# A hybrid SSD and retention block: squares on two engines, transposes in two parts, earlier weight loads, mixed rows behind passes, a halved last bank

## The chip, the core and the metric

The kernel runs on one core of a Trainium2 chip. The metric is the device time of one execution in microseconds (us). The engines of the core work side by side, each through its own queue in order, and wait for one another by semaphores: TensorE (PE in the profile: matrix products; PEld is its weight load), VectorE (DVE), ScalarE (ACT), GpSimd (POOL) and SyncE (SP, which here only issues DMAs). PSUM has eight banks of 128 x 512 f32 numbers in which PE accumulates.

## The reference

One layer on 512 tokens of width 2048, batch 1. All in f32:

```python
mod = silu(c) @ w_ada + b_ada                  # shift, scale, gate
u = rms_norm(x, norm_w) * (1 + scale) + shift
z, xbc, dt_raw, q, k, v, g = split(u @ w_in)   # 2048 x 11296
# SSD: conv of 4 taps and SiLU on xbc; 32 heads, 4 groups, chunks of 128
y_ssd = group_rms_norm((ssd_chunked(xs, softplus(dt_raw + dt_bias), a, bm, cm) + xs * d_skip) * silu(z))
# retention: 8 heads, rotary q and k, decay per head, chunks of 128
y_ret = head_group_norm(retention_chunked(rot(q), rot(k), v)) * silu(g)
h = x + gate * (concat(y_ssd, y_ret) @ w_out)  # 4096 x 2048
return rms_norm(h, final_norm_w)
```

## The kernel before

Every large product is done in three matmuls on numbers that are split in two: a value is cast to a rounded part `hi` (ACT), the rest `lo` is the difference (DVE or POOL), and `mm3` (L107 to L109) adds hi·hi, hi·lo and lo·hi in PSUM. The layer goes through these stages.

**Start-up.** SP loads x as eight tiles `xt` of 128 x 1024 (four row blocks `t`, two halves `h`). ACT squares each with a sum (L158), POOL makes a factor of each row block of the two sums (L160, L75, L76), DVE scales the two tiles (L163), PE transposes (L168) into one PSUM bank for each of 16 blocks `k` of the width, banks of the tags "mm" and "aux" (four each) in turn, and ACT copies the bank to `xT` (L171). `csb` (L137 to L143) is silu(c) on all partitions.

**Modulation.** For each of the 16 blocks `mod` takes two dot products `dot` (L189): DVE multiplies a 1 MB tile `ada` of the modulation matrix, 128 x 2048, with `csb` and sums. ACT reads the sums (L199, L200), applies shift and scale to `xT` (L202) and casts it to `uh` (L205); DVE takes the rest `ul` (L206).

**The split phase.** The first products begin while the modulation is still under way. Two groups of columns, A (B and C of groups 0 and 1, and half of xs 0) and B (z 0 and the other half of xs 0), each fill six banks, four "mm" and two "aux". So they take turns over the pairs of blocks that are ready, as PLAN (L32) lists them: B0, then A0 A1, B1 B2, A2 A3 A4, B3 B4 B5, A5 A6 A7, B6 B7. `seg` does the products of one pair. Behind a turn `spill` (L264) copies the six banks to SBUF (`pA`, `pB`), and the group's next turn copies them back (L234). `weights` loads a pair's two tiles with `load_w`: SP's DMA to `raw` (3 buffers), a cast to `hi` on ACT (L98; 128 x 1024 for z or B and C, 128 x 512 for xs; 4 buffers), and `lo` on POOL, for late pairs on DVE (L99).

**SSD and retention.** A `unit` is a pass: a product of all 16 blocks with 512 columns. Between passes the four SSD groups (`ssd_a`, `ssd_b`) and the four pairs of retention heads run. Each gives four blocks of rows of the mixed matrix, which `put_mix` transposes on PE into a bank `pT` (L339), copies to `m` on ACT (L341, ring "mo" of three), combines on POOL (L349 to L352) and stores in DRAM with five POOL DMAs. During a pass `trickle` (SSD) and `between` (retention) put other small jobs behind its weight loads. `block_sums` prepares sums of w_out in DRAM by DMA.

**Output phase.** The product with w_out is done by a scheme of seven products on half-size blocks: three sweeps over banks U and W, and a last loop (L846 to L855) that adds the product with T4 to U's four banks, one for each pair (q, t) of column and row half. Its last three weight tiles are held and then used bank by bank. `finish` (L723) multiplies a bank with the gate, adds x and squares (L731 to L734); `store` (L739) makes the factor of a row block (L742, L75, L76), scales its four tiles on DVE (L747) and ACT (L749), and stores them.

A scheduler sets the order on each engine: it takes the program's order with priorities and its own model of times, and so an engine's queue isn't simply the order in which the code is written. `issue_after` ties one instruction behind another.

## Time and profile before

| | before |
|---|---|
| median of 3 runs | 1471.01 us (1468.2 to 1472.3) |
| profiled execution, its own time | 1466.36 us |
| its span from first to last instruction | 1464.7 us |
| mean clock granted to TensorE | 0.992 |
| DVE, ACT, POOL busy | 59%, 40%, 26% |
| start-up, to the first product of the split phase | 32.67 us |
| last matmul begins | 1453.13 us |

A row of the timeline has its start and its length in us, engine, line, operation, tiles (output<-inputs), shapes and count; in brackets stands how long the engine was idle before it, and what released it. A row with x2 or more has several instructions. A matmul of 128 x 512 is shown with 0.39 us, but the next one starts 0.23 us after it: they overlap.

### The profile page before, as it was taken

To read this page: it belongs to the slowest core of one execution; us is meant where nothing else is said; L and a number is where in the kernel's file an instruction comes from. 1 tells how busy PE (TensorE), PEld (TensorE's weight loads), DVE (VectorE), ACT (ScalarE), POOL (GpSimd) and SP (SyncE) were. 2 spreads that over 40 slices of the span, in tenths; PEclk is the share of its full clock that TensorE was granted. 3 is DMA by queue.
4 is the path that set the end of the run, shared out by engine and by line. 5 is a ranking of instruction groups with operands and counts; after the bars stand their busy time and mean duration, and the time that the engine had idled before them with its cause. 6 is when DMAs were issued, how large, how long until landed. Compare 5 with 4: busy or idle time off the path is not lost.

```text
span 1464.7 us, 17212 instructions
## 1 busy us (share of the span) xinstructions
PE 1427.2 (97%) x6481; PEld 1169.5 (80%) x6481; DVE 861.6 (59%) x1008; ACT 579.1 (40%) x820; POOL 380.7 (26%) x440
## 2 busy tenths in 40 slices
PE   6999999899999999999999999999999999999996
PEld 4777888788888888888888888888888778888885
DVE  6888657866556555543554355435535556558585
ACT  7666543434424423221322132213222456446453
POOL 4433114566035335501430143023200300000000
PEclk9999999999999999999999999999999999999999
DMA  9997643566647847966697578666644698778755
GB/s 363 349 362 265 221 178 118 177 197 167 188 156 210 243 144 215 280 221 180 215 262 235 158 228 263 228 156 198 184 153 154 212 329 268 245 242 271 238 185 189
DMA packets 86262, 324.09 MB, mean 221 GB/s; under 512 B 11297, under 2 KB 11473, under 8 KB 81057
## 3 DMA queue, kind: packets, MB, share of 16 engines
q1 hardware_dynamic: 67858, 262.30, 51.3%
q0 software_dynamic: 17168, 58.59, 17.1%
q10 hardware_dynamic: 1152, 2.10, 0.4%
q8 instruction: 51, 0.84, 0.2%
q14 instruction: 33, 0.27, 0.1%
HBM read 304.00 MB, written 86.05 MB: 266 GB/s over the span
## 4 chain that ended last, share of the span: by engine, by line
PE 82%; issue 5%; DMA 5%; ACT 3%; DVE 3%; POOL 2%; SPq 0%; DVEq 0%; POOLq 0%; ACTq 0%
PE acc L109 17%; PE acc L107 17%; PE acc L108 17%; PE U L107 3%; PE U L109 3%; PE U L108 3%; PE W L109 2%; PE W L108 2%; PE W L107 2%; PE py L442 2%; PE A L107 1%; DMA raw<-w_out_d 1%; PE A L108 1%; DMA ada<-w_mod_d 1%; PE A L109 1%
## 5 line engine op out<-in xcount | busy, mean ns | idle before, releaser
L98 ACT CAST hi<-raw 128x1024 fp32r<-128x1024 f32 (+1 forms) x184 | 186.8, 1016 | 446.8 <-PE acc L109 221.5
L99 DVE TENSOR_TENSOR lo<-raw,hi 128x1024 fp32r<-128x1024 f32 (+1 forms) x166 | 212.4, 1285 | 226.5 <-ACT hi L98 226.0
L108 PE MATMUL acc<-lo,uh 128*128 128x512 f32 x704 | 277.2, 394 | 0.0
L107 PE MATMUL acc<-hi,uh 128*128 128x512 f32 x704 | 276.0, 394 | 0.0
L109 PE MATMUL acc<-hi,ul 128*128 128x512 f32 x704 | 275.4, 392 | 0.0
L109 PE MATMUL acc<-uh,lo 128*128 128x512 f32 x512 | 201.0, 393 | 0.0
L108 PE MATMUL acc<-ul,hi 128*128 128x512 f32 x512 | 200.1, 391 | 0.0
L107 PE MATMUL acc<-uh,hi 128*128 128x512 f32 x512 | 199.7, 392 | 0.0
L774 DVE TENSOR_TENSOR lo<-raw,hi 128x1024 fp32r<-128x1024 f32 x112 | 137.9, 1235 | 83.4 <-ACT hi L773 83.1
L773 ACT CAST hi<-raw 128x1024 fp32r<-128x1024 f32 x112 | 117.8, 1054 | 128.1 <-PE W L109 52.1
L108 PEld LDWEIGHTS acc<-lo,uh 128*128 128x128 f32 x704 | 132.8, 189 | 27.8 <-issue 0.5
L109 PEld LDWEIGHTS acc<-hi,ul 128*128 128x128 f32 x704 | 132.6, 188 | 28.0 <-issue 0.5
L107 PEld LDWEIGHTS acc<-hi,uh 128*128 128x128 f32 x704 | 132.8, 189 | 27.6 <-ACT cr L306 0.3
L109 PEld LDWEIGHTS acc<-uh,lo 128*128 128x128 f32 x512 | 96.2, 188 | 20.1 <-issue 0.7
L107 PEld LDWEIGHTS acc<-uh,hi 128*128 128x128 f32 x512 | 96.2, 188 | 20.0 <-issue 0.7
L108 PEld LDWEIGHTS acc<-ul,hi 128*128 128x128 f32 x512 | 96.2, 188 | 19.6
L613 DVE SCALAR_TENSOR_TENSOR gacc<-graw,cs,gacc 128x512 f32<-128x512 f32 x60 | 47.5, 792 | 90.9 <-DMA graw<-w_gate_d 90.1
L108 PE MATMUL U<-lo,mh 128*128 128x512 f32 x256 | 100.0, 391 | 0.5 <-DVE lo L774 0.5
L109 PE MATMUL U<-hi,ml 128*128 128x512 f32 x256 | 99.6, 390 | 0.0
L107 PE MATMUL U<-hi,mh 128*128 128x512 f32 x256 | 95.5, 391 | 0.1
L189 DVE SCALAR_TENSOR_TENSOR ada<-ada,csb 128x2048 f32<-128x2048 f32 x32 | 90.5, 2855 | 0.8 <-DMA ada<-w_mod_d 0.8
L75 POOL TENSOR_SCALAR rs<-rs 128x1 f32<-128x1 f32 x4 | 2.1, 522 | 283.6 <-DVE rs L742 283.5
(238 smaller groups left out, 2255.2 us busy)
## 6 DMA issues: line engine op xcount, KB each, us to landing
ada<-w_mod_d SPq DMA_DIRECT2D x32, 1024.0 KB, 7.1
T<-w_out_d SPq DMA_DIRECT2D x64, 512.0 KB, 5.8
raw<-T SPq DMA_DIRECT2D x64, 512.0 KB, 4.3
raw<-w_out_d SPq DMA_DIRECT2D x48, 512.0 KB, 4.4
raw<-w_in_z SPq DMA_DIRECT2D x32, 512.0 KB, 4.1
T<-w_out_d POOLq DMA_DIRECT2D x32, 512.0 KB, 8.7
T<-T POOLq DMA_DIRECT2D x32, 512.0 KB, 14.7
raw<-w_in_qk SPq DMA_DIRECT2D x32, 512.0 KB, 4.2
```

The lines of the kernel that those rows point to most:

```text
L75: pool.tensor_scalar(dst, src, scale, eps, ALU.mult, ALU.add)
L98: act.copy(hi, raw)
L99: eng.tensor_tensor(lo, raw, hi.bitcast(F32), ALU.subtract)
L107: pe.matmul(dst, lhsT=ah, rhs=bh, start=first, stop=False, skip_group_check=more)
L108: pe.matmul(dst, lhsT=ah, rhs=bl, start=False, stop=False, skip_group_check=more)
L109: pe.matmul(dst, lhsT=al, rhs=bh, start=False, stop=last, skip_group_check=more)
L189: dve.scalar_tensor_tensor(ada, ada, 0.5, csb, ALU.mult, ALU.mult, accum_out=dst)
L442: pe.matmul(py[:, hd], lhsT=dec[:, h, :], rhs=xd[:, hd], start=True, stop=True)
L613: dve.scalar_tensor_tensor(gacc, raw[:, kk, :], cs[:, k:k + 1], gacc, ALU.mult, ALU.add)
L773: act.copy(dst[0], src)
L774: dve.tensor_tensor(dst[1], src, dst[0].bitcast(F32), ALU.subtract)
```

## The change

There are five parts.

1. Squares of the second half-tiles (h = 1) go from ACT to DVE, each half with its own `junk` buffer.
2. The transposes become a function `transposed(k)`: eight of them, then the first modulation and the weights of B0, whose cast is tied behind the first `uh` cast, and then the other eight.
3. The weights of the next turn's first pair are loaded in the code before the turn's spills.
4. The mixed rows of the SSD groups go to a list, `to_mix`; `mix_one` takes one off in the passes that follow, from their third weight tile on. The last two blocks `m` come from the ring "cbt".
5. In the last loop five weight tiles are held (LATE), the last bank is done in two halves of 256 columns, and row block 3 has finishing code of its own.

```diff
...
 ADAB = 4
 RING = 12
 EPS = 1e-6
+LATE = 5
 PLAN = [("B", [0]), ("A", [0, 1]), ("B", [1, 2]), ("A", [2, 3, 4]),
         ("B", [3, 4, 5]), ("A", [5, 6, 7]), ("B", [6, 7])]
 COL_Z, COL_XS, COL_B, COL_C, COL_DT = 0, 2048, 4096, 4608, 5120
...
 
     last_load = [None]
 
-    def load_w(src, width, eng=dve):
+    def load_w(src, width, eng=dve, after=None):
         raw = wp.tile([P, 2, width], F32, tag="raw", bufs=3, name="raw")
         last_load[0] = sp.dma_start(raw.rearrange("p k f -> p (k f)"), src)
         hi = wp.tile([P, 2, width], F32R, tag="hi", bufs=4, name="hi")
         lo = wp.tile([P, 2, width], F32R, tag="lo", bufs=4, name="lo")
-        act.copy(hi, raw)
+        with tc.issue_after(after) if after is not None else nullcontext():
+            act.copy(hi, raw)
         eng.tensor_tensor(lo, raw, hi.bitcast(F32), ALU.subtract)
         return hi, lo
 
...
     rst = const.tile([P, NC], F32, name="rst")
     for t in range(NC):
         for h in range(2):
-            junk = sp0.tile([P, HD], F32, tag="junk", bufs=1, name="junk")
-            act.activation(junk, xa[t][h], AF.Square, accum_out=ss[:, t, h:h + 1])
+            junk = sp0.tile([P, HD], F32, tag=f"junk{h}", bufs=1, name="junk")
+            if h == 0:
+                act.activation(junk, xa[t][h], AF.Square, accum_out=ss[:, t, h:h + 1])
+            else:
+                dve.scalar_tensor_tensor(junk, xa[t][h], 1.0, xa[t][h], ALU.mult, ALU.mult,
+                                         accum_out=ss[:, t, h:h + 1])
         r = rst[:, t:t + 1]
         pool.tensor_tensor(r, ss[:, t, 0:1], ss[:, t, 1:2], ALU.add)
         rsqrt_into(r, r, 1.0 / D, EPS)
         for h in range(2):
             dve.tensor_scalar(xa[t][h], xa[t][h], r, None, ALU.mult)
     xT = []
-    for k in range(NK):
+
+    def transposed(k):
         pt = bank("mm" if k % 2 else "aux", "pt")
         for t in range(NC):
             pe.transpose(pt[:, t * P:(t + 1) * P],
...
         ada = sp0.tile([P, D], F32, tag="ada", bufs=ADAB, name="ada")
         sp.dma_start(ada, w_mod[2 * k + m])
         dve.scalar_tensor_tensor(ada, ada, 0.5, csb, ALU.mult, ALU.mult, accum_out=dst)
+
+    last_split = [None]
 
     def mod(k0, nk):
 
...
             act.activation(xT[k], xT[k], AF.Identity, bias=sh, scale=sc)
             h_k = up.tile([P, L], F32R, tag="uh", bufs=NK, name=f"uh{k}")
             l_k = up.tile([P, L], F32R, tag="ul", bufs=NK + 1, name=f"ul{k}")
-            act.copy(h_k, xT[k])
+            last_split[0] = act.copy(h_k, xT[k])
             dve.tensor_tensor(l_k, xT[k], h_k.bitcast(F32), ALU.subtract)
             uh.append(h_k)
             ul.append(l_k)
...
 
     early = {}
 
-    def weights(which, p):
-        return [load_w(w_in[nm][p], wd, lo_eng(which, p)) for n, (nm, wd) in enumerate(ranges[which])]
+    def weights(which, p, after=None):
+        return [load_w(w_in[nm][p], wd, lo_eng(which, p), after)
+                for n, (nm, wd) in enumerate(ranges[which])]
 
     def seg(which, p, first, last):
         again = first and part[which][0] is not None
...
             act.copy(part[which][b], cur[which][b])
 
     plan = PLAN
+    for k in range(NK // 2):
+        transposed(k)
     mod(0, 1)
-    early["B", 0] = weights("B", 0)
+    early["B", 0] = weights("B", 0, last_split[0].ins)
+    for k in range(NK // 2, NK):
+        transposed(k)
     mod(1, 1)
     ready = 1
     last_of = {w: max(i for i, (v, _) in enumerate(plan) if v == w) for w in "AB"}
...
                 ready += 1
             seg(which, p, j == 0, j == len(pairs) - 1)
         if i != len(plan) - 1:
+            nxt = plan[i + 1][0], plan[i + 1][1][0]
+            early[nxt] = weights(*nxt)
             spill(which)
     start.close()
 
...
         return ap.rearrange("p (h d) -> p h d", h=HPG)
 
     half_of = {}
+    to_mix = []
+
+    def mix_one(kc):
+
+        if kc >= 2 and to_mix:
+            put_mix(*to_mix.pop(0))
 
     def put_mix(i, src, nw):
 
...
         pT = bank("aux", "pT")
         for c in range(NC):
             pe.transpose(pT[:, c * P:(c + 1) * P], src[c], ident)
-        m = t2k("mo", 3, "m")
+        m = t2k("cbt", 2, "m") if i >= 30 else t2k("mo", 3, "m")
         act.activation(m, pT, AF.Copy, scale=nw)
         if i % 2 == 0:
             half_of["m"] = m
...
     def trickle(kc):
         if kc % 2:
             copy_one()
+        mix_one(kc)
 
     def block_sums():
 
...
             act.activation(zss[c], y, AF.Square, accum_out=sq[:, c:c + 1])
             rsqrt_into(sq[:, c:c + 1], sq[:, c:c + 1], 1.0 / 2048.0, EPS)
             dve.tensor_scalar(y, y, sq[:, c:c + 1], None, ALU.mult)
-        for i in range(4):
-            put_mix(4 * g + i, [y[:, i * P:(i + 1) * P] for y in ys], hv(V_SNW, 4 * g + i))
+        to_mix.extend((4 * g + i, [y[:, i * P:(i + 1) * P] for y in ys], hv(V_SNW, 4 * g + i))
+                      for i in range(4))
 
 
     def rotary(pb, name):
...
             gate_part(i // 24, i // 3 % 8)
         else:
             copy_one()
+        mix_one(kc)
 
     def gate_part(n, q):
         raw = wp.tile([P, 2, 512], F32, tag="raw", bufs=3, name="graw")
...
         if j % 2 == 0:
             m = mixed(mixd["A22"][j // 2])
         held.append((j, m, weight(T4(j))))
-        if NJ - 3 <= j < NJ - 1:
+        if NJ - LATE <= j < NJ - 1:
             continue
         for at in PAIRS:
-            for j_, m_, w in held:
-                mul(bu, m_, j_ % 2, w, False, j_ == NJ - 1, True, [at])
+            q, t = at
+            parts = (slice(0, 256), slice(256, 512)) if j == NJ - 1 and at == PAIRS[-1] else \
+                (slice(0, 512),)
+            for cols in parts:
+                for j_, m_, (wh, wl) in held:
+                    sl = slice(j_ % 2 * 256 + t * P, j_ % 2 * 256 + (t + 1) * P)
+                    mm3(bu[at][:, cols], (m_[0][:, sl], m_[1][:, sl]),
+                        (wh[:, q, cols], wl[:, q, cols]), False, j_ == NJ - 1, True)
         held = []
-    for t in range(2):
-        for q in range(2):
-            finish(2 + t, 2 * q, bu[q, t])
-        store(2 + t)
+    for q in range(2):
+        finish(2, 2 * q, bu[q, 0])
+    store(2)
+
+
+
+    ssl = const.tile([P, 5], F32, name="ssl")
+    last = {}
+    for i, (n, lo_, hi_) in enumerate(((0, 0, 512), (2, 0, 256), (2, 256, 512))):
+        cols = slice(lo_, hi_)
+        if lo_ == 0:
+            xr = t2k("zs", 4, "xr")
+            sp.dma_start(xr, x[3 * P:4 * P, n * 512:(n + 1) * 512])
+            h = up.tile([P, 512], F32, tag="uh", bufs=NK, name=f"h3_{n}")
+            hout[3][n] = h
+        dve.tensor_tensor(h[:, cols], bu[n // 2, 1][:, cols], gate[n][:, cols], ALU.mult)
+        dve.tensor_tensor(h[:, cols], h[:, cols], xr[:, cols], ALU.add)
+        jk = res.tile([P, 512], F32, tag="jk", bufs=1, name="jk")
+        act.activation(jk[:, cols], h[:, cols], AF.Square, accum_out=ssl[:, i:i + 1])
+        dve.tensor_tensor(h[:, cols], h[:, cols], fws[n][:, cols], ALU.mult)
+    act.copy(ssl[:, 3:5], sso[:, 3, 1::2])
+    rs = small.tile([P, 1], F32, name="rs")
+    dve.tensor_reduce(rs, ssl, mybir.AxisListType.X, ALU.add)
+    rsqrt_into(rs, rs, 1.0 / D, EPS)
+    for m in range(4):
+        h = hout[3][m]
+        if m % 2 == 0:
+            dve.tensor_scalar(h, h, rs, None, ALU.mult)
+        else:
+            act.activation(h, h, AF.Copy, scale=rs)
+        (sp if m % 2 == 0 else act).dma_start(out[3 * P:4 * P, m * 512:(m + 1) * 512], h)
 
 
 def _tables():
```

On DVE, at the start-up: L189 and L196 are the dot products of `ada`, L143 and L145 make `csb`, L163 of before and L169 of the change scale the tiles `xt` (two for a row block), and L163 of the change, with `junk,ss`, is a square. Before:

```order
L143 SCALAR_TENSOR_TENSOR csb<-csb,pc 128x512 x2
L163 TENSOR_SCALAR xt_119<-xt_119,rst 128x1024
L163 TENSOR_SCALAR xt_121<-xt_121,rst 128x1024
L163 TENSOR_SCALAR xt_123<-xt_123,rst 128x1024
L163 TENSOR_SCALAR xt_125<-xt_125,rst 128x1024
L163 TENSOR_SCALAR xt_127<-xt_127,rst 128x1024
L163 TENSOR_SCALAR xt_129<-xt_129,rst 128x1024
L189 SCALAR_TENSOR_TENSOR ada,raw_md<-ada,csb 128x2048 x4
L206 TENSOR_TENSOR ul_301<-xT_174,uh_300 128x512
```

And after the change, from the third square on:

```order
L163 SCALAR_TENSOR_TENSOR junk,ss<-xt_125 128x1024
L169 TENSOR_SCALAR xt_119<-xt_119,rst 128x1024
L169 TENSOR_SCALAR xt_121<-xt_121,rst 128x1024
L169 TENSOR_SCALAR xt_123<-xt_123,rst 128x1024
L169 TENSOR_SCALAR xt_125<-xt_125,rst 128x1024
L163 SCALAR_TENSOR_TENSOR junk,ss<-xt_129 128x1024
L196 SCALAR_TENSOR_TENSOR ada,raw_md<-ada,csb 128x2048
L169 TENSOR_SCALAR xt_127<-xt_127,rst 128x1024
L169 TENSOR_SCALAR xt_129<-xt_129,rst 128x1024
L196 SCALAR_TENSOR_TENSOR ada,raw_md<-ada,csb 128x2048 x2
```

The last square stands in front of the first dot product, and that dot product now in front of the last two scalings, where all four dot products stood behind them.

On ACT, from the end of turn A1 to the start of B1: L98 and L100 are casts of weights, L264 and L274 spill A, L234 and L244 restore B, L199 to L205 and L208 to L214 are the modulation. The 128 x 1024 cast in each piece is that of z for B1. Before:

```order
L98 CAST hi<-raw 128x1024
L200 ACTIVATE md<-raw_md,bsc,vec 128x1
L202 ACTIVATE xT_202<-xT_202,md 128x512
L205 CAST uh_484<-xT_202 128x512
L264 COPY pA_555<-A_419 128x512
L264 COPY pA_557<-A_420 128x512
L234 COPY B_567<-pB_407 128x512
L264 COPY pA_559<-A_421 128x512
L234 COPY B_568<-pB_409 128x512
L264 COPY pA_561<-A_422 128x512
L264 COPY pA_563<-A_423 128x512
L234 COPY B_569<-pB_411 128x512
```

After the change:

```order
L211 ACTIVATE xT_210<-xT_210,md 128x512
L274 COPY pA_567<-A_431 128x512
L214 CAST uh_484<-xT_210 128x512
L274 COPY pA_569<-A_432 128x512
L244 COPY B_579<-pB_419 128x512
L274 COPY pA_571<-A_433 128x512
L100 CAST hi<-raw 128x1024
L274 COPY pA_573<-A_434 128x512
L244 COPY B_580<-pB_421 128x512
L274 COPY pA_575<-A_435 128x512
L208 ACTIVATE md<-raw_md,vec 128x1
L274 COPY pA_577<-A_436 128x512
```

The cast stood ahead of the modulation of that block and of all the spills; it stands now behind three spills and the first restore.

On DVE, at the end of the program: the tiles h of row block 3 (before 11212 and 11219, now 11228 and 11236). L731 and L901 multiply a bank U with the gate, L732 and L902 add x, L742, L766 and L908 sum the squares, L747, L771 and L913 scale, and L905 multiplies with the final weight. Before:

```order
L731 TENSOR_TENSOR h_0_11212<-U,gate_8647 128x512
L742 TENSOR_REDUCE rs<-sso 128x1
L732 TENSOR_TENSOR h_0_11212<-h_0_11212,xr 128x512
L747 SCALAR_TENSOR_TENSOR h_0_11186<-h_0_11186,rs,fw_8760 128x512
L747 SCALAR_TENSOR_TENSOR h_2_11193<-h_2_11193,rs,fw_9158 128x512
L731 TENSOR_TENSOR h_2_11219<-U,gate_8651 128x512
L732 TENSOR_TENSOR h_2_11219<-h_2_11219,xr 128x512
L742 TENSOR_REDUCE rs<-sso 128x1
L747 SCALAR_TENSOR_TENSOR h_0_11212<-h_0_11212,rs,fw_8760 128x512
L747 SCALAR_TENSOR_TENSOR h_2_11219<-h_2_11219,rs,fw_9158 128x512
```

After the change:

```order
L901 TENSOR_TENSOR h_0_11228<-U,gate_8647 128x512
L766 TENSOR_REDUCE rs<-sso 128x1
L902 TENSOR_TENSOR h_0_11228<-h_0_11228,xr 128x512
L771 SCALAR_TENSOR_TENSOR h_0_11201<-h_0_11201,rs,fw_8760 128x512
L771 SCALAR_TENSOR_TENSOR h_2_11208<-h_2_11208,rs,fw_9158 128x512
L905 TENSOR_TENSOR h_0_11228<-h_0_11228,fw_8760 128x512
L901 TENSOR_TENSOR h_2_11236<-U,gate_8651 128x256 x2
L902 TENSOR_TENSOR h_2_11236<-h_2_11236,xr 128x256 x2
L905 TENSOR_TENSOR h_2_11236<-h_2_11236,fw_9158 128x256 x2
L908 TENSOR_REDUCE rs<-ssl 128x1
L913 TENSOR_SCALAR h_0_11228<-h_0_11228,rs 128x512
L913 TENSOR_SCALAR h_2_11236<-h_2_11236,rs 128x512
```

The scaling of row block 2 (L771) now stands ahead of the last bank's work in full, and the two halves of each step of the last bank stand next to each other.

## The prediction

> **What bounds the kernel now.** I read the page first, then TensorE's waits, then the row-by-row timeline around each wait. The first line below is the page's: TensorE (PE) is busy for 97% of the span. The others are the waits of the PE queue: us in total, times, longest.
>
> ```profile
> PE 1427.2 (97%) x6481; PEld 1169.5 (80%) x6481; DVE 861.6 (59%) x1008; ACT 579.1 (40%) x820; POOL 380.7 (26%) x440
> ...
> PE B L107 <- ACT uh L205: 5.8, 1, 5.8
> PE pt L168 <- DVE xt L163: 4.3, 4, 2.8
> PE pT L339 <- DVE y L447: 4.2, 1, 4.2
> ...
> PE A L107 <- ACT hi L98: 3.1, 2, 2.8
> PE B L107 <- ACT hi L98: 2.0, 1, 2.0
> PE B L107 <- ACT B L234: 0.8, 1, 0.8
> PE pT L339 <- DVE y L480: 0.7, 1, 0.7
> PE W L107 <- ACT m L341: 0.6, 1, 0.6
> PE U L108 <- DVE lo L774: 0.5, 1, 0.5
> PE W L107 <- ACT hi L773: 0.5, 1, 0.5
> ```
>
> The kernel is bound by its matmuls, and the change removes none of them. What it can gain is in these waits, and in the start and the tail, where PE has nothing to do. All the waits shown sum to 22.5 us. So each edit is worth one row of this table, or less, and I take them in the order of the program.
>
> **Start-up.** The next rows are from the timeline: start, us, then engine and line. They run from the squares to the first split matmul. The first row is a group with the minimum, median and maximum in ns.
>
> ```profile
> L143 DVE SCALAR_TENSOR_TENSOR csb<-csb,pc x4: 680/689/690, 8.5 to 14.3; 128x512 f32<-128x512 f32 x4
> 9.91 1.05 ACT L158 ACTIVATE junk<-xt 128x1024 f32<-128x1024 f32 x1
> 20.08 1.42 DVE L163 TENSOR_SCALAR xt<-xt,rst 128x1024 f32<-128x1024 f32 x2 [0.99 <-POOL rst L76]
> 21.40 4.50 ACT L171 COPY xT<-pt 128x512 f32<-128x512 f32 x9 [2.58 <-PE pt L168]
> 21.41 2.29 DVE L189 SCALAR_TENSOR_TENSOR ada<-ada,csb 128x2048 f32<-128x2048 f32 x1
> 27.32 1.15 ACT L98 CAST hi<-raw 128x1024 fp32r<-128x1024 f32 x1
> 28.55 8.50 POOL L99 TENSOR_TENSOR lo<-raw,hi 128x1024 fp32r<-128x1024 f32 x3 [8.51 <-ACT hi L98]
> 28.97 4.16 DVE L189 SCALAR_TENSOR_TENSOR ada<-ada,csb 128x2048 f32<-128x2048 f32 x1 [0.19 <-DMA ada<-w_mod_d]
> 31.96 0.66 ACT L205 CAST uh<-xT 128x512 fp32r<-128x512 f32 x1
> 32.67 0.80 PE L107 MATMUL B<-hi,uh 128*128 128x512 f32 x1 [5.79 <-ACT uh L205]
> ```
>
> Before, ACT sets the pace with eight squares, and the last scaling ends on DVE at 20.08 + 1.42 = 21.5. After the change DVE has four squares as well. No row has a square on DVE. The nearest is a dot product of the same instruction (row 21.41): 2.29 us for 2048 columns, so 1.14 for 1024. The bounds are 0.71, one scaling of the same width in row 20.08, and 2.29. I take 1.14, because form and operands are those of the dot product.
>
> DVE's order after the change also puts the first dot product ahead of the last two scalings. From the second x tile (9.91) DVE then holds 4 squares (4.6), 8 scalings (5.7), three csb products (2.1) and one dot (2.3): 14.7 us, and with some 0.5 in which it waits for the first scale factor it ends at 25.1, against 21.5. That is 3.6 us later for the last scaled tile. Part comes back: ACT now needs eight copies and not sixteen before it turns to the first modulation. Last input of the first copies near 24.4, copies from 24.9, eight at 0.5 (4.50 for 9) to 28.9, modulation and uh cast to 30.4, the B0 casts (1.15 and about half that) to 31.9. The first B bank is the bank of a transpose of the second eight, so two more copies come first: 32.9, and its first matmul stands near 33.2 against 32.67. The next three banks come free only every 1.0 us behind it, and the second uh cast comes after all eight copies. The dot products behind the first stand (25.1 - 23.7) = **1.4 us later**. I put the end of turn B0 1.5 us later (bounds -1.5, if DVE never sets the pace, and +3.5, if nothing of the 3.6 comes back).
>
> The Trainium skill speaks against this edit: "Vector Engine (DVE) Microarchitecture Reference", section 7, says that this family of instructions with two non-bf16 SBUF sources runs at half throughput, since no port is left for the accumulator. By that sentence a square would take some 2 x 1.14 us. Row 21.41 has two f32 SBUF sources and an accumulator, and ran 2048 columns in 2.29 us, one column in 1.12 ns, so I read the trace as disagreeing, and keep the doubled square as a rival.
>
> **The turns.** Between two turns ACT spills six banks, restores six, and casts the next weights; PE needs the first restored bank and the cast.
>
> ```profile
> 32.00:63.00 31.00, 29.51 (x119) 23.28 (x119) 30.55 (x22) 17.52 (x33) 17.21 (x6) 0.91 0.94 370
> 53.34 1.03 ACT L98 CAST hi<-raw 128x1024 fp32r<-128x1024 f32 x1
> 60.52 0.63 ACT L205 CAST uh<-xT 128x512 fp32r<-128x512 f32 x1
> 62.66 0.50 PE L107 MATMUL B<-hi,uh 128*128 128x512 f32 x1 [0.82 <-ACT B L234]
> 82.14 1.09 ACT L98 CAST hi<-raw 128x1024 fp32r<-128x1024 f32 x1
> 83.28 0.50 PE L107 MATMUL A<-uh,hi 128*128 128x512 f32 x1 [2.81 <-ACT hi L98]
> 141.35 0.50 PE L107 MATMUL A<-uh,hi 128*128 128x512 f32 x1 [0.25 <-ACT hi L98]
> ```
>
> The first row is the window 32 to 63 us: busy time of PE, weight loads, DVE, ACT and POOL, the clock, the DMA share, GB/s. **DVE is busy 30.55 of 31.00 us** there: the chain of dot products is a second bound, and what makes it later is passed on.
>
> Writing the load ahead of the spills does not put the cast ahead of them at every turn; ACT's order decides.
> - A1 to B1: before, the 128x1024 cast ran at 53.34, long ahead. Now it stands behind three spills and a restore. With ACT held by the uh cast of the modulation (60.52) as before, three copies of 0.5 follow it and the cast would start near 62.7, as PE started at 62.66, and end at 63.8. The products with lo wait for POOL behind that, 2.8 us each by the row of three (8.50), while those without lo run, and the later restores come behind the cast. I take +2.1 (bounds 0, and +3.9: cast and POOL in full).
> - B2 to A2: the cast moves ahead of two spills and a restore, three copies at 0.5, so 82.14 becomes 80.6. Of the 2.81 us wait 1.6 goes (bounds 0 and 2.8). POOL's lo part is late next.
> - A4 to B3: the cast stays behind all six spills, and the 2.0 us of the table stay: 0 (bounds -2.0 and 0).
> - B5 to A5: the cast now stands between the copies; the wait of 0.25 becomes about one cast: +0.7 (bounds 0 and 0.85).
>
> The moved loads go through SP's queue ahead of dot-product loads that came first until now. The DMA share is already 0.94, and bytes do not change: 1 MB at 370 GB/s is 2.8 us that one dot product could be late, or early; I count 0, since DVE is the later of the two.
>
> **The mixed rows.** The rows are TensorE's largest single wait behind the start, one matmul 2.5 us after it, and ACT's longest wait at the start of the output phase.
>
> ```profile
> 264.60 0.69 PE L339 MATMUL pT<-ident,y 128*128 128x128 f32 x2 [4.19 <-DVE y L447]
> 267.07 0.63 PE L108 MATMUL acc<-lo,uh 128*128 128x512 f32 x1
> 1163.80 0.69 ACT L341 ACTIVATE m<-pT,half 128x512 f32<-128x512 f32 x1 [6.67 <-DMA mixAS<-m]
> ```
>
> The wait of 4.19 us, with some 2 us of slow clock behind it (matmuls of 0.63), belongs to group 0. There the order of the transposes on PE and of the work on DVE is the same before and after: **0**. The rows of groups 2 and 3 do go behind passes: the 0.7 us on L480 goes. Their POOL sums and five DMAs each are only read 600 us later, so nothing waits. At the start of the output phase the last copies come from another ring, so ACT no longer stands 6.67 us for a DMA; the three PE waits behind it (0.6 + 0.5 + 0.5) go: -1.6 (bounds -2.5 and 0).
>
> **The tail.**
>
> ```profile
> 1447.44 0.69 DVE L731 TENSOR_TENSOR h<-U,gate 128x512 f32<-128x512 f32 x1 [6.07 <-PE U L109]
> 1452.90 0.39 PE L108 MATMUL U<-lo,mh 128*128 128x512 f32 x1
> 1453.13 0.39 PE L109 MATMUL U<-hi,ml 128*128 128x512 f32 x1
> 1453.65 1.41 DVE L747 SCALAR_TENSOR_TENSOR h<-h,rs,fw 128x512 f32<-128x512 f32 x2 [0.72 <-POOL rs L76]
> 1454.98 0.68 DVE L731 TENSOR_TENSOR h<-U,gate 128x512 f32<-128x512 f32 x1
> 1457.24 0.16 DVE L742 TENSOR_REDUCE rs<-sso 128x1 f32<-128x4 f32 x1 [0.85 <-ACT jk L734]
> 1458.34 1.42 DVE L747 SCALAR_TENSOR_TENSOR h<-h,rs,fw 128x512 f32<-128x512 f32 x2 [0.94 <-POOL rs L76]
> ```
>
> Before, DVE's scaling of row block 2 (1453.65) holds back the last bank until 1454.98. With five weights held, that scaling falls under matmuls. The two halves do not overlap: DVE's order has both gate products next to each other, and the second needs the last matmul. From 1453.6 then: two half products and two half adds (0.37 each, half of 0.68 and a little) to 1455.1, half a square and its read-out to 1455.8, the reduce, and 1.10 us from reduce to scaling as before (1457.24 to 1458.34): 1456.9 against 1458.3, **-1.4** (bounds -2.0 and 0). The 30 half matmuls take as long as 15 whole ones of 0.23 us, plus 0.1; at worst a half takes as long as a whole one, +3.4. The last held weight must be ready 12 matmuls into the first bank, near 1442.4; DVE was done with it at 1447.44 - 6.07 = 1441.4, so 1 us is left.
>
> **The sum.** +1.5 + 2.1 - 1.6 + 0 + 0.7 + 0 - 0.7 - 1.6 - 1.4 + 0.1 = -0.9. Against the profiled execution (1466.36 us) that is 1465.5; that execution lies 4.65 below the median of the runs (1471.01), so on the scale of the median **1470.1, say 1470**. A difference of 0.3%, 4.4 us, is about what a measurement of this kernel can tell from no change, so this is a forecast of no change: gains at the tail and the output phase are paid back in the first 150 us.
>
> **Rivals.**
> 1. *The start and the casts come early, as the code reads.* If DVE does not set the pace, B0 ends 1.5 earlier, A1 to B1 costs nothing, B2 to A2 gains 2.8: the other turns give 0, and the later terms -3.6 as above. The sum is -7.9 and the time 1463. For it: four squares less are 4.2 us of ACT. Against it: DVE's order, and the 30.55 of 31.00. Chance 0.18. That the stall of group 0 also goes, -6.3, gives 1464; the unchanged order speaks against it: 0.05.
> 2. *The chain of dot products becomes the bound.* The dot products slow down when POOL subtracts (4.16 at 28.97 against 2.29 at 21.41). In the window with no slack POOL has six instructions; each can cost DVE up to 1.9 to 2.2 us. If four of them newly fall on dot products, the chain is 8 us late, not 1.4. ACT has, in its own queue, the reading of a dot product (L200) now ahead of the last two spills of B2, so the gain of 1.6 there goes too: 1470 + 6.6 + 1.6 = 1478, slower. It decides once the chain is more than about 4 us late. For it: 17.21 us of POOL in that window. Against it: POOL's work is not more than before, and it lay on dot products already. Chance 0.25.
> 3. *The square on DVE takes 2.29*: 4.6 later, 1474.7, chance 0.04. *Half matmuls cost as much as whole ones*: +3.3, 1473.4, chance 0.05. Both still count as no change.
>
> **How the numbers follow.** The forecast has 0.43 and the cases of 3. have 0.09: same 0.52. Rival 1 and the group 0 case give faster 0.23, rival 2 slower 0.25. The range reaches from 1463, rival 1, to 1478, rival 2, which takes in the bounds of the terms, of which not all end on one side. The likeliest case's own range is 1466 to 1475.
>
> **What would show it.** Right: in the profile after, the first B matmul starts at 32.5 to 34.5, a dot product stands ahead of the last scaling, the wait of the first B1 matmul on the cast is new and 1 to 3 us, that of A2 is down to about 1, the 4.2 us of group 0 is still there, ACT's 6.67 us is gone, and the last reduce begins under 3 us behind the start of the last matmul, where it was 1457.24 - 1453.13 = 4.1. Wrong: a first B matmul before 31, or PE waits of over 5 us between 50 and 85 us.

## The result, and the profile after

The changed kernel takes **1478.09 us** (median of 4 runs, 1477.26 to 1479.76), against 1470.66 for the kernel before (4 runs, 1468.2 to 1472.3). The ratio is 1.0053, with a 95% interval of 1.0036 to 1.0071: it is slower by half a percent, where I had forecast 1470, no change, and a range that ended at 1478.

First the waits of TensorE's queue in the profile after, to be laid beside those of before. L109 to L111 are now the lines of `mm3`, L100 and L101 the cast and the lo part of a weight tile, L175 the transposes, L361 those of the mixed rows.

```profile
PE pt L175 <- DVE xt L169: 7.7, 4, 3.8
PE B L110 <- POOL lo L101: 6.1, 4, 1.8
PE pT L361 <- DVE y L470: 4.6, 1, 4.6
...
PE acc L109 <- ACT cr L322: 2.9, 3, 2.4
PE A L109 <- ACT hi L100: 2.1, 3, 1.2
PE A L111 <- POOL lo L101: 2.0, 1, 2.0
PE B L109 <- ACT xT L178: 2.0, 1, 2.0
PE B L109 <- ACT hi L100: 1.9, 2, 1.2
```

Two names are new and large: waits on POOL's lo parts, 8.1 us where there were none, and a wait on `cr`, the copy that the convolution makes of a bank. The waits on `hi` are smaller, those of the output phase (on m, hi, lo) are gone, and the 4.6 us of group 0 is still there. Of the 8.1 us, 5.4 fall in turns A2 to A4 and B3 to B5, and 2.7 in turns B0 and B1.

The timeline says when each place was reached. In this table, worked out from the start of one matmul in each line, the last column is what the profiled execution after had lost by then against the first profile of before.

| reached, us | before | after | lost |
|---|---|---|---|
| first product of turn B0 | 32.7 | 33.8 | 1.1 |
| first product of turn A0, A1 | 44.2 | 47.8 | 3.6 |
| of turn A2 to A4 | 83.3 | 87.6 | 4.4 |
| of turn B3 to B5 | 112.6 | 120.3 | 7.8 |
| of turn A5 to A7 | 141.3 | 153.9 | 12.5 |
| last product of the split phase | 182.5 | 195.1 | 12.5 |
| last product of the heads' passes | 1141.7 | 1157.7 | 16.0 |
| 400 matmuls into the output phase | 1239.4 | 1251.9 | 12.5 |
| last matmul | 1453.1 | 1465.9 | 12.8 |
| end of the span | 1464.7 | 1476.8 | 12.1 |

So there are two losses, 12.5 us in the split phase and some 4 us in the SSD passes (0.9 of it comes back behind groups 2 and 3), and one gain of 3.5 at the start of the output phase. The two profiles show more (12.1 us) than the medians (7.4), because the first profile of before was an execution of 1466.4, faster than the usual one. Much of the difference lies in the split phase, as the first run below shows.

The start-up, from the timeline of the profile after: two of the squares and the dot product behind the last one on DVE, the sum for the last scale factor on POOL, the last scaling, the first copies and the first product.

```profile
9.35 1.31 DVE L163 SCALAR_TENSOR_TENSOR junk<-xt 128x1024 f32<-128x1024 f32 x1
13.30 1.22 DVE L163 SCALAR_TENSOR_TENSOR junk<-xt 128x1024 f32<-128x1024 f32 x1
...
21.38 2.29 DVE L196 SCALAR_TENSOR_TENSOR ada<-ada,csb 128x2048 f32<-128x2048 f32 x1
21.61 2.11 POOL L166 TENSOR_TENSOR rst<-ss 128x1 f32<-128x1 f32 x1 [2.73 <-DVE junk L163]
24.67 1.42 DVE L169 TENSOR_SCALAR xt<-xt,rst 128x1024 f32<-128x1024 f32 x2 [0.99 <-POOL rst L77]
25.99 4.01 ACT L178 COPY xT<-pt 128x512 f32<-128x512 f32 x8 [1.98 <-PE pt L175]
33.77 0.50 PE L109 MATMUL B<-uh,hi 128*128 128x512 f32 x1 [1.99 <-ACT xT L178]
```

The sum of two numbers takes POOL 2.11 us. It ends at 23.72, just behind the dot product on DVE (21.38 + 2.29 = 23.67); without one it takes 0.19. So the dot product stands ahead of the last scaling not only in DVE's queue: it also holds up the factor that this scaling waits for.

Within turn A2 to A4 and turn B3 to B5 the same picture comes twice. The rows are from the timeline of the profile after: a modulation step that waits for a dot product, the cast behind it, two lo parts on POOL (128 x 1024 and 128 x 512), and PE's wait.

```profile
94.88 0.39 ACT L209 ACTIVATE md<-raw_md,bsc,vec 128x1 f32<-128x1 f32 x1 [3.44 <-DVE ada L196]
96.67 1.04 ACT L100 CAST hi<-raw 128x1024 fp32r<-128x1024 f32 x1
97.79 7.58 POOL L101 TENSOR_TENSOR lo<-raw,hi 128x1024 fp32r<-128x1024 f32 x2 [5.70 <-ACT hi L100]
102.13 0.73 PE L111 MATMUL A<-uh,lo 128*128 128x512 f32 x2 [2.01 <-POOL lo L101]
...
127.11 0.39 ACT L209 ACTIVATE md<-raw_md,bsc,vec 128x1 f32<-128x1 f32 x1 [3.59 <-DVE ada L196]
128.90 1.05 ACT L100 CAST hi<-raw 128x1024 fp32r<-128x1024 f32 x1
130.03 7.57 POOL L101 TENSOR_TENSOR lo<-raw,hi 128x1024 fp32r<-128x1024 f32 x2 [5.71 <-ACT hi L100]
134.36 0.50 PE L110 MATMUL B<-lo,uh 128*128 128x512 f32 x1 [1.83 <-POOL lo L101]
```

ACT idles for 3.4 and 3.6 us in front of a step that isn't needed yet (of block 8, which pair A4 uses, and of block 12, which the next turn uses), and the cast that is needed stands behind it. Then POOL takes 7.6 us for two tiles, since dot products run on DVE all the while. In the profile before, the cast for A3 stood ahead of such a step:

```profile
86.53 1.04 ACT L98 CAST hi<-raw 128x1024 fp32r<-128x1024 f32 x1
87.64 4.33 POOL L99 TENSOR_TENSOR lo<-raw,hi 128x1024 fp32r<-128x1024 f32 x1 [0.68 <-ACT hi L98]
```

There the lo part was as slow on POOL, 4.33 us, but it began 4.4 us behind the turn's first matmul and not 10.2, and PE waited for no lo part.

### The profile page after: what moved, and what is told of

Same layout as the page of the kernel before. It is cut to its first block, busy times and chain, and to the rows that moved or that the text cites. A ratio compares the mean times of both kernels' runs of the same rounds, so it can differ in the third digit from the quotient of the medians.

```text
span 1476.8 us, 17247 instructions
## 1 busy us (share of the span) xinstructions
PE 1430.9 (97%) x6496; PEld 1171.5 (79%) x6496; DVE 864.5 (59%) x1021; ACT 573.9 (39%) x815; POOL 380.5 (26%) x440
## 4 chain that ended last, share of the span: by engine, by line
PE 85%; POOL 5%; issue 4%; DMA 3%; DVE 2%; ACT 1%; POOLq 0%; ACTq 0%; DVEq 0%
PE acc L109 18%; PE acc L111 17%; PE acc L110 17%; PE U L109 4%; PE U L111 4%; PE U L110 4%; PE W L110 3%; PE W L111 3%; PE W L109 3%; POOL lo L101 2%; PE py L465 1%; PE B L110 1%; PE B L111 1%; PE B L109 1%; PE po L562 1%
## 5 line engine op out<-in xcount | busy, mean ns | idle before, releaser
L100 ACT CAST hi<-raw 128x1024 fp32r<-128x1024 f32 (+1 forms) x184 | 186.7, 1016 | 449.1 <-PE acc L111 227.2
L101 DVE TENSOR_TENSOR lo<-raw,hi 128x1024 fp32r<-128x1024 f32 (+1 forms) x166 | 214.8, 1298 | 231.8 <-ACT hi L100 231.1
L109 PE MATMUL acc<-hi,uh 128*128 128x512 f32 x704 | 275.8, 394 | 0.2 <-ACT cr L322 0.2
L111 PE MATMUL acc<-hi,ul 128*128 128x512 f32 x704 | 275.1, 391 | 0.0
L109 PE MATMUL acc<-uh,hi 128*128 128x512 f32 x512 | 200.7, 394 | 2.8 <-ACT cr L322 2.8
L111 PE MATMUL acc<-uh,lo 128*128 128x512 f32 x512 | 201.0, 393 | 0.0
L111 PEld LDWEIGHTS acc<-hi,ul 128*128 128x128 f32 x704 | 132.6, 188 | 28.1 <-issue 0.5
L109 PEld LDWEIGHTS acc<-hi,uh 128*128 128x128 f32 x704 | 132.5, 188 | 27.5 <-ACT cr L322 0.4
L109 PEld LDWEIGHTS acc<-uh,hi 128*128 128x128 f32 x512 | 96.1, 188 | 23.6 <-ACT cr L322 3.6
L111 PEld LDWEIGHTS acc<-uh,lo 128*128 128x128 f32 x512 | 96.1, 188 | 20.5 <-issue 0.7
L110 PE MATMUL U<-lo,mh 128*128 128x512 f32 (+1 forms) x261 | 100.4, 385 | 0.0
L111 PE MATMUL U<-hi,ml 128*128 128x512 f32 (+1 forms) x261 | 100.4, 385 | 0.0
L109 PE MATMUL U<-hi,mh 128*128 128x512 f32 (+1 forms) x261 | 97.1, 386 | 0.0
L196 DVE SCALAR_TENSOR_TENSOR ada<-ada,csb 128x2048 f32<-128x2048 f32 x32 | 83.9, 2652 | 0.0
```

Of the source, the lines that this page charges most:

```text
L100: act.copy(hi, raw)
L101: eng.tensor_tensor(lo, raw, hi.bitcast(F32), ALU.subtract)
L109: pe.matmul(dst, lhsT=ah, rhs=bh, start=first, stop=False, skip_group_check=more)
L110: pe.matmul(dst, lhsT=ah, rhs=bl, start=False, stop=False, skip_group_check=more)
L111: pe.matmul(dst, lhsT=al, rhs=bh, start=False, stop=last, skip_group_check=more)
L196: dve.scalar_tensor_tensor(ada, ada, 0.5, csb, ALU.mult, ALU.mult, accum_out=dst)
```

## The experiments

Two theories stood against each other for the split phase. One: what costs is the order, casts behind modulation steps and lo parts that POOL does slowly and just in time. The other: the late start is passed on, because the chain of dot products is the bound. All ratios are to the kernel before, with 95% intervals.

**The same kernel again.** No edit.

> The kernel before, unchanged, for a second profile. The first profiled execution (1466.4 us) is shorter than all four timed ones (1468.2 to 1472.3). If that was chance, this profile lies near 1470, with the same waits in the split phase (end of the split products near 182.9) and its extra 3 to 5 us elsewhere; if the split phase itself varies from one execution to the next, its end moves by several us, and the +12.5 us that the two profiles show there is partly chance. Ratio to before 1.000.

1469.49 us, ratio 1.0000 (0.9990 to 1.0009). Its profile reached turn A2 at 84.6 and ended the split products at 184.0, 1.5 us later than the first profile, with all instructions in the same order. The next run and the first ring run below have the same order in that phase too, and ended them at 186.2 and 188.0. So one profile of this phase is good to about 3 us, and what the change loses there lies between 7 and 12.5 us. The waits are steadier than the ends: from the first product of A2 to that of A5, PE's waits sum to 2.7 to 3.6 us in these four profiles and to 9.3 in the profile after; in the whole phase to 6.4 to 7.1 and 13.2. The rest of the spread is slow matmuls, 3.3 to 8.0 us in the four and 6.9 after.

**Mixed rows and tail alone.** Squares, transposes and loads go back:

```diff
-            if h == 0:
-                act.activation(junk, xa[t][h], AF.Square, accum_out=ss[:, t, h:h + 1])
-            else:
-                dve.scalar_tensor_tensor(junk, xa[t][h], 1.0, xa[t][h], ALU.mult, ALU.mult, ...)
+            act.activation(junk, xa[t][h], AF.Square, accum_out=ss[:, t, h:h + 1])
...
-            nxt = plan[i + 1][0], plan[i + 1][1][0]
-            early[nxt] = weights(*nxt)
```

> Only the mixed rows behind passes and the halved last bank; squares, transposes and loads as before. My theory: the loss sits in two places, the split phase (+12.5 us in the profile, from squares and transposes) and the pass behind group 1 (+4.2, from mixed rows: the fourth m waits for a buffer of the ring of three in front of the conv copies on ScalarE). Then the split products end near 182.9, a wait of 2 to 3 us on the conv copies stands in the pass behind group 1, the output phase starts without waits, and the time is 1469 to 1471. Rival, the second loss only follows from the late split phase: no such wait, and 1465 to 1467.

1469.41 us, ratio 1.0001 (0.9992 to 1.0010), as my theory had it. The loss of the change is in the first three parts. And in the pass behind group 1 ACT has this row, in the timeline of this run:

```profile
364.50 0.69 ACT L356 ACTIVATE m<-pT,half 128x512 f32<-128x512 f32 x1 [5.48 <-DMA mixAS<-m]
```

The group's fourth block m waits 5.5 us for a buffer of the ring of three, that is for the store of the first, and the copies of convolution banks stand behind it; PE waits 2.1 us for them. Before the change the fourth m stood behind these copies. It is the wait that the change takes away from the start of the output phase, put into an earlier pass.

**Without the mixed rows.** `put_mix` is called at once, as before, and all m come from the ring of three.

> The change without its mixed-rows part (mixed rows where they were before, all blocks m from the ring of three); the rest as changed. My theory: the split phase is as in the change (+12.5 at its end against the first profile), the +4.2 behind group 1 goes, and the waits at the L480 rows (0.7) and at the start of the output phase (1.6 to 3.4) come back: about 1 us under the change, 1476 to 1478. Rival, the mixed rows cost nothing by themselves: 2 to 4 us over the change, 1480 to 1482.

1478.77 us, ratio 1.0067 (1.0052 to 1.0082): 0.7 more than the change, less than these runs can tell, and between the two forecasts. The mixed rows part loses in the SSD passes and gains in the output phase, and both are nearly equal.

**Dot products behind the last scaling.** In the change:

```diff
-            dve.tensor_scalar(xa[t][h], xa[t][h], r, None, ALU.mult)
+            scaled = dve.tensor_scalar(xa[t][h], xa[t][h], r, None, ALU.mult)
...
-        dve.scalar_tensor_tensor(ada, ada, 0.5, csb, ALU.mult, ALU.mult, accum_out=dst)
+        with tc.issue_after(scaled.ins):
+            dve.scalar_tensor_tensor(ada, ada, 0.5, csb, ALU.mult, ALU.mult, accum_out=dst)
```

> The change, with the dot products tied behind the last scaling, so that no dot product runs on VectorE while GpSimd makes the last row block's factor. My theory of the start: the factor's add took 2.1 us and not 0.2 because of that dot product, which also stands ahead of the scaling; the first copy of a transpose then starts near 22.5 to 23 and not 26.0, the first product of the split phase near 30.5 to 31. For the split phase: if lateness at the start is what costs (rival), the whole 12.5 us shrinks by 6 or more and the time is 1470 to 1472; if the new order of casts behind modulation steps is what costs (my theory), only 1 to 3.5 us go and the time is 1475 to 1477.

1476.62 us, ratio 1.0048 (1.0032 to 1.0065). The timeline of this run has the sum at its short length:

```profile
21.27 0.19 POOL L166 TENSOR_TENSOR rst<-ss 128x1 f32<-128x1 f32 x1 [2.74 <-DVE junk L163]
23.73 4.02 ACT L178 COPY xT<-pt 128x512 f32<-128x512 f32 x8 [6.03 <-PE pt L175]
```

0.19 and not 2.11, and the first copies 2.3 us earlier. But of this only 1.5 us is left at the end by the medians, and the intervals of the two ratios overlap. The start is not what costs most.

**Squares back on ACT**, the other parts as changed; and **transposes back in one part**, with the squares on two engines.

> The change with all squares on ScalarE again; transposes in two parts, mixed rows and halved bank stay. In this order the cast for pair A3 stands ahead of a modulation step again, while the casts for the first B1 and A2 products stand behind all spills. My theory (casts and the lo parts behind them set the split phase, the start only a few us of it): last scaling ends near 21.5 again, no wait on a lo part in turn A2 to A4, split products end at 187 to 190, time 1471 to 1474. Rival, squares on VectorE are the whole loss: split end 183 to 185 and 1468 to 1469. Rival, the two-part transposes are the whole loss: as the change, 1477 to 1479.

> The change with the sixteen transposes in one part and the first cast untied, squares still on two engines. Here the cast for A3 stands behind two uh casts, so by my theory the waits on GpSimd's lo parts stay: 5 to 8 us in all, split end 191 to 196, time 1475 to 1479. Rival, the two-part transposes are the whole loss: split end near 184, 1468 to 1470.

Squares back: 1469.37 us, ratio 0.9995 (0.9985 to 1.0004). Transposes back: 1473.08 us, ratio 1.0019 (1.0007 to 1.0031). Both came out faster than I expected, the first one by its number nearer to its rival, the squares as the whole loss. The two-part transposes alone cost nothing that shows, the squares alone 3.7 us (against the 1469.4 of tail and mixed rows alone), and both together 8.7. The profiles tell how little the start matters: the first product came at 30.2 with squares back, at 37.7 with transposes back, and turn A2 began at 85.9 and 84.6. What differs is behind that, and it is not how late the cast comes. With squares back turn B3 to B5 took 29.0 us, with transposes back 33.7, in the change 33.5; the cast for B4 begins 8.6 us behind the turn's first matmul in all three. But POOL took 4.9 us for the two lo parts behind it with squares back, where one dot product ran on DVE beside them, and 6.5 with transposes back and 7.6 in the change, where two did. The row is from the timeline with squares back:

```profile
124.64 4.94 POOL L101 TENSOR_TENSOR lo<-raw,hi 128x1024 fp32r<-128x1024 f32 x2 [5.72 <-PE B L111]
```

So a late cast alone does not cost; a late cast with slow lo parts behind it does.

**The early loads.** With and without those two lines the scheduler gives the same instructions in the same order on all five queues. This part of the change does nothing.

**Casts first.** In the change, a pair's weights are loaded ahead of the modulation that follows, and its first small step on ACT is tied behind the pair's last cast; in a second kernel, both small steps are:

```diff
+            if (which, p) not in early:
+                early[which, p] = weights(which, p)
             while ready < min(p + 2, NK // 2):
...
+            with tc.issue_after(last_cast[0].ins) if last_cast[0] is not None else nullcontext():
-            act.activation(sh, raw_md[:, 0:1], AF.Identity, ...)
+                act.activation(sh, raw_md[:, 0:1], AF.Identity, ...)
```

> The change, with the weights of a pair loaded ahead of the modulation of the blocks that follow, and that modulation's first step on ScalarE tied behind the pair's last cast. The start (to the end of B0) stays as it is. My theory: the waits on lo parts in turns A2 to A4 and B3 to B5 (6 us in the profile of the change) go or fall under 2, split end 188 to 191, time 1471 to 1474. Rival, the chain of dot products is the bound and the casts only wait beside it: the waits change their name (uh or ul instead of lo) and the time stays 1477 to 1480.

> As the run with casts first, but both of the modulation's small steps (L199 and L200 of before) are tied behind the pair's casts; in that run only one was, and the cast for B4 still stood behind a step that waited 4.5 us for a dot product. My theory: in turn B3 to B5 the cast for B4 then starts near 120 to 122 and not 129, its lo part ends before it is needed, and the turn takes 29 to 31 us and not 33.6; turn A2 to A4 stays at 30 to 32, because there the uh casts are needed at once (the waits only change their name); split end 190 to 192, time 1473 to 1476. Rival, the order of casts does not matter in either turn: B3 to B5 stays at 33 or more, time 1477 to 1479.

One step tied: 1477.70 us, ratio 1.0039 (1.0023 to 1.0054); nothing gained, and the cast for B4 still stood behind the other step, which waited 4.5 us. Both tied: 1474.77 us, ratio 1.0027 (1.0015 to 1.0039), 3.3 less than the change. That is inside the expected range, but by luck, since it came the other way round than expected. Turn A2 to A4 fell from 32.7 to 29.5 us, where I had expected it to stay; turn B3 to B5, where I had expected the gain, took 34.2. There the four lo parts followed one another on POOL without a gap, and the modulation that had been pushed back was late instead. First POOL's timeline in that turn of the second kernel:

```profile
115.36 13.01 POOL L102 TENSOR_TENSOR lo<-raw,hi 128x1024 fp32r<-128x1024 f32 x4 [18.33 <-ACT hi L101]
```

And PE's waits in the same run:

```profile
PE B L111 <- POOL lo L102: 4.4, 3, 1.6
...
PE dtb L266 <- ACT uh L217: 2.9, 2, 1.8
```

13.0 us for two tiles of each size: alone they take 2.4 and 1.3 us, 7.4 together. So the order of casts is one part of the loss, and POOL's speed another.

**Lo parts of pairs 3 and 4 on DVE**, in the change. Up to turn B3 the casts keep their order, so in effect only the engine is tried:

```diff
-        return dve if which == "A" and p >= 4 or p >= 5 else pool
+        return dve if p >= 3 else pool
```

> The change, with the lo parts of pairs 3 and 4 (A3, B3 and B4, six tiles) on VectorE like those of later pairs; ScalarE's order up to turn B3 stays as in the change. Port theory: these lo parts are late because on GpSimd they wait for the dot product that runs on VectorE (4.3 us against 2.4); on VectorE they take 1.2 and 0.7. Then the waits on lo parts in turns A2 to A4 and B3 to B5 (6 us) fall under 3, turn A2 to A4 takes 30 to 31 us and not 32.7, B3 to B5 30 to 31.5 and not 33.6, split end 189 to 192, time 1472.5 to 1475. Rival: the lo parts then stand behind dot products in VectorE's own queue and delay later ones; the same waits under other names, 1476 to 1479.

1472.14 us, ratio 1.0008 (0.9998 to 1.0018): **6.0 us less** than the change, slightly more than expected, and no longer told from before. The timeline of this run, the casts of A3 and B4 and their lo parts:

```profile
95.71 1.04 ACT L100 CAST hi<-raw 128x1024 fp32r<-128x1024 f32 x1
96.78 1.23 DVE L101 TENSOR_TENSOR lo<-raw,hi 128x1024 fp32r<-128x1024 f32 x1
...
125.42 1.04 ACT L100 CAST hi<-raw 128x1024 fp32r<-128x1024 f32 x1
126.50 1.23 DVE L101 TENSOR_TENSOR lo<-raw,hi 128x1024 fp32r<-128x1024 f32 x1
```

Both casts come as late in their turns as in the change (9.0 and 8.7 us behind the turn's first matmul, there 9.0 and 8.6), but the first lo part is done in 1.2 us. Turn A2 to A4 took 30.1 us, turn B3 to B5 29.2, the waits on lo parts in them are gone, and the split products ended at 187.3.

**Start and casts together**: the ties of both mends in one kernel.

> The change with both mends so far: dot products behind the last scaling, and both modulation steps behind the pair's casts. If the two add up, split end 187 to 190 and time 1472 to 1474 (1.5 and 3.3 us under the change's 1478.1); if the start is absorbed by turn A2 whatever it is, only the second counts: 1474 to 1476.

1474.46 us, ratio 1.0032 (1.0017 to 1.0046), the same as with the casts alone. The two do not add up; the start is taken up by turn A2.

**Towards a better kernel.** Squares, transposes and loads as before the change, halved bank, mixed rows behind passes, and the fourth m of each SSD group from the ring "cbt" too; then with casts first; then with two-part transposes and not casts first; then this with the lo parts of pairs 3 and 4 on DVE:

```diff
-        m = t2k("cbt", 2, "m") if i >= 30 else t2k("mo", 3, "m")
+        m = t2k("cbt", 2, "m") if i >= 30 or i < 16 and i % 4 == 3 else t2k("mo", 3, "m")
```

> Squares, transposes and loads as before the change; halved last bank; mixed rows behind passes, but each SSD group's fourth block m from the ring cbt too, so that it does not wait for the first one's store in front of the conv copies. My theory of the second loss: the waits on conv copies (2.5 us in the run with only tail and mixed rows) fall under 0.5, and the time is 1466 to 1467.5, better than both kernels. Rival, the transposes in the pass cost by themselves: 1469 to 1470, as in that run.

> The best kernel so far (squares, transposes and loads as before the change, mixed rows with the ring cbt, halved last bank) with the same tie of both modulation steps behind casts. There the casts stood ahead already in most places, so by my theory little is left to gain: 1465 to 1467, the same as without it. Rival, casts first is worth something by itself: 1461 to 1464.

> The same best kernel with the transposes in two parts (squares on ScalarE). First product of the split phase near 30 and not 33, as in the run with squares back. If an earlier start is worth anything here, 1463 to 1465; if the start of turn A2 is set by the modulation whatever the start (my theory: it was 84 to 86 in four runs whose first product came between 30.2 and 37.7), 1465.5 to 1467.5.

> The best kernel with transposes in two parts (squares on ScalarE, ring cbt, halved bank), with the lo parts of pairs 3 and 4 on VectorE. In its profile PE waits 2.7 us for lo parts. Port theory: 1.5 to 3 us less than that kernel's 1464.9, 1462 to 1463.5. Rival: no gain, 1464 to 1466.

| kernel | us | ratio | interval |
|---|---|---|---|
| ring cbt | 1466.11 | 0.9962 | 0.9948 to 0.9976 |
| and casts first | 1464.73 | 0.9963 | 0.9950 to 0.9976 |
| ring cbt, transposes in two parts | 1464.85 | 0.9961 | 0.9948 to 0.9973 |
| and lo parts of pairs 3 and 4 on DVE | **1461.25** | 0.9942 | 0.9925 to 0.9960 |

With the ring, the four m run without a break in the pass behind group 1 (timeline of the first of these), and PE has no wait on the convolution copies left there:

```profile
352.92 2.42 ACT L356 ACTIVATE m<-pT,half 128x512 f32<-128x512 f32 x4 [1.28 <-PE pT L354]
355.21 0.61 ACT L315 COPY cr<-acc 128x512 f32<-128x512 f32 x1
```

That is worth 3.3 us against tail and mixed rows alone. Casts first and two-part transposes add nothing that these runs can tell; the median with two-part transposes lies in the range of an earlier start being worth something, but the ratios are 0.9962 without them and 0.9961 with them. The lo parts on DVE add 3.6: in this kernel's profile turn A2 to A4 takes 28.0 us and B3 to B5 27.3, where 116 matmuls at 0.2275 are 26.4. It is the fastest of all, 9.5 us under before by the medians of one timing.

## Why the prediction was wrong

**The step that failed** is the part on the turns. I priced what lies at the borders of turns, a cast among spills, and put A4 to B3 at 0 and B5 to A5 at +0.7. The loss came inside the turns, where the prediction had no term: A3's and B4's casts stand behind modulation steps in ACT's order, and the lo parts behind them, now just in time, run on POOL at 3.8 us a tile. Turn A2 to A4 took 32.7 us against 29.3 in the first two profiles of before, and turn B3 to B5 33.5 against 28.8 and 29.0. The other two profiles of that order have up to 32.1 and 31.0, but mostly by slow matmuls; in PE's waits between A2 and A5 all four agree, at 2.7 to 3.6 us against 9.3. The order of ACT could have told the first half; the second half stood in the row of 8.50 us for three tiles, which I used at one border only.

**Rival 2** gave the right time, 1478, by luck, and half of the mechanism. DVE and POOL do hold each other up, but it was not the chain of dot products that grew: the 32 dot products took 84.9 us after and 91.4 before, summed from their rows. The price fell on the other side, on POOL's lo parts, which before had been done early enough for nobody to wait. The run with lo parts on DVE shows it: 6.0 us.

**The start.** The square took 1.22 us (1.31 the first), where I had 1.14; the half throughput that the Trainium skill states for such operands ("Vector Engine (DVE) Microarchitecture Reference", section 7) did not come: the trace disagrees. DVE ended the last scaling at 24.67 + 1.42 = 26.1 and not 25.1: I had left out POOL's sum, 2.11 us because of the dot product. The first product came at 33.77 where I had 33.2, but the end of B0 was 3.6 us late and not 1.5. How much that is worth I had too high all the same: a first product 1.6 us earlier brought at most 1.5 us, one 0.8 us earlier nothing in the other pairing, and turn A2 began between 83.3 and 87.6 in all profiles, with first products from 30.0 to 37.7.

**A1 to B1 and B2 to A2.** Together I had +0.5, and the profile has +0.8: with B0, A2 began 4.4 us late against the first profile, 3.1 against the second one. The new cast stall in B1 is there, though as 0.7 us at the first matmul and 1.2 at the lo part behind it; the old one of A2 is wholly gone, where I had left 1.2 us of it.

**That a part does nothing** stood among none of my rivals. The early loads, which give the change one of its five names, leave every queue as it was. I had read the casts' new places as their effect.

**The mixed rows.** Right: group 0's wait is still there (4.2 and now 4.6 us), and the output phase starts without waits. There I had -1.6 and the profiles show -3.5. The wait of 0.7 us at 573.7 (L480) is gone as well, but one as long is new at group 1, at 344.7 us (L503). Wrong: that nothing waits for the moved rows. The fourth m, in front of the convolution's copies, cost PE 2.4 us at once and some 4 us in that pass:

```profile
374.03 0.69 ACT L363 ACTIVATE m<-pT,half 128x512 f32<-128x512 f32 x1 [5.72 <-DMA mixAS<-m]
375.24 0.50 PE L109 MATMUL acc<-uh,hi 128*128 128x512 f32 x1 [2.37 <-ACT cr L322]
```

I had listed what is behind the moved step's DMAs, but not what is behind its copies on ACT.

**The tail.** -1.4 was forecast. The rows of the profile after, from DVE's products with the gate to the scaling:

```profile
1465.93 0.28 PE L111 MATMUL U<-hi,ml 128*128 128x256 f32 x1
1466.72 0.75 DVE L901 TENSOR_TENSOR h<-U,gate 128x256 f32<-128x256 f32 x2
1468.44 0.96 DVE L905 TENSOR_TENSOR h<-h,fw 128x256 f32<-128x256 f32 x2 [0.30 <-ACT jk L904]
1469.32 0.15 DVE L908 TENSOR_REDUCE rs<-ssl 128x1 f32<-128x5 f32 x1
1470.42 0.88 DVE L913 TENSOR_SCALAR h<-h,rs 128x512 f32<-128x512 f32 x2 [0.95 <-POOL rs L77]
```

From the start of the last matmul to the scaling it is 4.5 us, against 5.2 before: -0.7; to the reduce it is 3.4, where I had said under 3. The first product waits for a multiplication of the bank ahead of it, and the reduce stands behind the two multiplications with the final weight, which overwrite h and so wait for ACT's squares. The halves cost little, as forecast: 0.12 us from one half matmul to the next.

So the sum came out at -0.9 where it was +7.4: two terms were missing, casts and lo parts inside turns and the m in front of the convolution copies; the others were off by some 2 us or less against the first profile.

What stays open: why squares and two-part transposes together cost 8.7 us, and 3.7 and 0 each alone. The lo parts behind B4's cast, 7.6 us in the change against 6.5 and 4.9, point to how dot products fall on them, but why they fall so was not tried. The two parts change the order of ACT's queue in many places at once, and only the two causes above were tried one by one. Of the 8.7, 6.0 went with the lo parts, which also covers part of the casts' 3.3.

## What to carry to other kernels

A change that is meant for one stage moves a scheduler's order in all of them: read every wait that a queue's new order makes, within stages as well as at their borders, and compare the order with and without each part, since a part may do nothing. An engine's instruction that waits for something not yet needed makes late what stands behind it; so put into the list, for each moved step, what is behind it on each engine that it uses. A helper engine that is slow beside a busy neighbour is free only as long as its results are early; when they come just in time, give them to the faster engine, though it is the fuller one.

## What the runs showed of the hardware

A sum of 128 x 1 on GpSimd took 2.11 us while a dot product of 128 x 2048 ran on VectorE, and 0.19 when none did; a subtraction of 128 x 1024 took 2.4 us alone and up to 4.4 beside dot products. The dot products grew in the same way, from 2.28 to 4.46. The same queues, in four profiles, ended the split phase at 182.5, 184.0, 186.2 and 188.0 us; most of the difference is TensorE's slow pace of 0.43 us a matmul behind short waits, which by the rows (start to start, above 0.2275 us, without the waits) took 3.3 us of the phase in the first profile and 8.0 in the last. The same wait does not always bring it: behind the 2.8 us ahead of turn A2 the matmuls followed at 0.23 us in the first profile, with a granted clock of 1.00 up to 90 us, and eleven times at 0.43 in the last, with 0.51.
